# Five more seven-product pairs in the mixing stage of a hybrid decoder layer

## The chip, the cores and the metric

The kernel runs on one core of a Trainium2 chip. The metric is device time in microseconds, the median of several runs; lower is better. TensorE (PE) multiplies matrices, VectorE (DVE) and ScalarE (ACT) do elementwise work, GpSimd (POOL) issues small DMAs here, SyncE (SP) issues the loads of the weights.

## The reference

One decoder layer for 256 tokens of width 2048, in float32:

```
x = x + 1/2 * SwiGLU_1(RMSNorm(x))            # 2048 -> 5632 twice, 5632 -> 2048
z = RMSNorm(x) @ W_in                         # q, k, v and gates of two head groups
o_g = gated linear attention (4 heads), normed, times silu(r)
o_a = dilated attention (8 heads): q and k normed per head, rotary, three windows merged
x = x + concat(o_g, o_a) @ W_out              # 2048 -> 2048
x = x + 1/2 * SwiGLU_2(RMSNorm(x))
```

The weights are far larger than the activations: all in all 350 MB of them are loaded, each once.

## The kernel before, in words

**Products in three parts.** Each float32 weight tile is split into a rounded part (`wh`, made on ACT, L114) and a remainder (`wl`, made on DVE, L115), and so is each activation tile (`hh` and `hl`, or `oah`, `oal`, `ogh`, `ogl`). A product is the sum of three matmuls: high by high (L277), high activation by low weight (L279), low by high (L281). Tokens come in two row tiles of 128 (`t`), output columns in blocks of 512 in pairs (`j`), and the depth in tiles of 128 (`k`), which are loaded in pairs (`kp`): one load of 1 MB brings two depth tiles by two column blocks into a `raw` buffer (three of them).

**Plain pairs.** `column_pair` runs 16 depth tiles into four PSUM banks. One depth tile is one job: a `wh`/`wl` tile of 1024 columns, then 2 x 2 x 3 = 12 matmuls of 512 columns. A pair of depth tiles is 24 matmuls.

**Sevens.** For a pair of depth tiles the two row tiles, two depth tiles and two column blocks make a 2 x 2 by 2 x 2 product of blocks. `seven_products` computes it with seven block products instead of eight (21 matmuls instead of 24), from sums of activation blocks and sums of weight blocks. The sums of activations are made by `seven_forms` (DVE, then a split). The sums of weights are made by `seven` (L234 on), in four parts, "plain", "last", "sums" and "more", each of which gives one `wh`/`wl` tile ("last" only half a tile, in a room of its own). Four of the seven products go to four further PSUM banks (`ms`), which a list of "fold" operations brings to the results after the last seven of the pair: in the output pairs `fold_into_xs` adds them to the residual `xs` with one ACT copy and eight DVE operations.

**Order of the weights.** A list of jobs (L182 to L186) holds all weight tiles in the order of their use. `weights` makes tiles until three are ready; there are four `wh` and four `wl` buffers (`WBUF`). `_order` turns a text such as "ssgsgsss" into an order of plain pairs (s) and sevens (g); the sevens take the first depth pairs, the plain ones the rest. Before the change, ten of the eleven column blocks of a feed-forward part have two sevens each ("ssgssgss"), the down projections have six sevens each, the second output pair has two ("ssgsgsss"), and q, k, v, the gates' projections and the first output pair have none.

**Work beside the matmuls.** `later` is a list of small pieces (rotary turns, scores, gated attention, norms) of which a few run before each step of matmuls, by a plan of `span` steps. A second list (`held`) keeps the ends of the norm blocks until the last seven of the second output pair, because they write the rows of `hh` and `hl` that hold the sums of activations (`lent`). The program is written in this order; the framework then orders each engine's instructions by its own estimate of when they are ready, so pieces move against each other. Waits between engines are semaphores that it sets.

**The stages around the change,** from the trace: q from 676 us, k from 721, v from 763, a narrow projection, three projections for the gated attention, the first output pair from 959, the second from 1005, the second feed-forward part from 1045. During the k pair DVE turns q by its rotary table (`rotate`, L628 to L634). At the end of a pair, `store` writes the banks out scaled (ACT, L651). In the first output pair the first eight depth tiles are attention (`oah`, `oal`), the other eight gated attention (`ogh`, `ogl`), which `gated` finishes in that same stage (L866, L867, transposes L110). After the first output pair, `out_evac` adds the banks to `xs` (L895) and `renorm` starts the norm of these columns: a transpose in 32 x 32 blocks, 16 DMAs for each of four blocks on GpSimd's queue (L136), and later `finish` (L156).

## Time and profile before

| what | value |
|---|---|
| median of 3 runs | 1718.4 us (1717.45 to 1718.85) |
| span of the profiled execution | 1715.9 us |
| PE busy | 1705.4 us, 99%, 7974 matmuls |
| DVE busy | 1416.9 us, 83% |
| ACT busy | 947.1 us, 55% |
| POOL busy | 505.7 us, 29% |
| loads of weights | 350.25 MB, 57.2% of the 16 DMA engines |
| chain that ended last | PE 89%, DMA 4%, DVE 4% |

The profiled execution is one run, and the profile gives its span from the first to the last instruction, which leaves out what lies around it. In rows of the trace a tile is written as `out<-in`, with buffer numbers left out; a number in brackets after a row is the idle time of the engine before it and what ended that. The mean duration of an instruction contains some overlap with its neighbours.

### The profile page before, as it was taken

What the parts mean: (1) busy time and instruction counts of PE and PEld (TensorE: products, weight loads), DVE (VectorE), ACT (ScalarE), POOL (GpSimd) and SP (SyncE); (2) the same over time, 40 slices, a digit from 0 to 9 for tenths busy, and PEclk for the clock granted to TensorE, in tenths of its full rate; (3) what the DMA queues carried; (4) which work ended last, traced back from release to release, by engine and by line L of the source; (5) the groups of instructions that cost most, each with busy time, mean ns of one, the idle gap of its engine ahead of it and who ended that gap; (6) DMA issues with size and microseconds to landing.
All of it is one profiled execution on the core that took longest, in us unless ns stands there. A gap on an engine that the chain in (4) does not pass through costs nothing.

```text
span 1715.9 us, 22309 instructions
## 1 busy us (share of the span) xinstructions
PE 1705.4 (99%) x7974; PEld 1485.1 (87%) x7974; DVE 1416.9 (83%) x1731; ACT 947.1 (55%) x1173; POOL 505.7 (29%) x1002
## 2 busy tenths in 40 slices
PE   9999999999999999999999999999999999999999
PEld 7888888888888888888888888888888888888887
DVE  6888889898898788577865788788888898898876
ACT  7555555555555555564654555555555555555453
POOL 0333334344410611054250043333333333420000
PEclk9999999999999999999999999999999999999999
DMA  8666666556665657577564467666666666665654
GB/s 345 213 229 224 219 211 232 208 213 236 234 250 219 217 203 244 192 237 235 195 210 172 148 198 269 210 231 225 222 224 220 226 212 224 218 242 222 248 204 147
DMA packets 85807, 378.62 MB, mean 221 GB/s; under 512 B 21392, under 2 KB 38800, under 8 KB 42688
## 3 DMA queue, kind: packets, MB, share of 16 engines
q1 hardware_dynamic: 50864, 350.25, 57.2%
q0 software_dynamic: 34112, 25.88, 5.3%
q8 instruction: 62, 1.02, 0.2%
q10 hardware_dynamic: 720, 1.07, 0.2%
q14 instruction: 49, 0.40, 0.1%
HBM read 354.57 MB, written 4.19 MB: 209 GB/s over the span
## 4 chain that ended last, share of the span: by engine, by line
PE 89%; DMA 4%; DVE 4%; POOL 1%; issue 1%; ACT 0%; DVEq 0%; SPq 0%; ACTq 0%; POOLq 0%
PE acc L279 20%; PE acc L277 20%; PE acc L281 20%; PE tp L281 4%; PE tp L277 4%; PE tp L279 4%; PE acc L303 4%; PE acc L304 4%; PE acc L302 4%; DVE wl L115 2%; DMA raw<-in_w_dn_dram 2%; DMA hh<-us 1%; PE tp L303 1%; PE tp L304 1%; PE tp L302 1%
## 5 line engine op out<-in xcount | busy, mean ns | idle before, releaser
L114 ACT ACTIVATE wh<-raw 128x1024 fp32r<-128x1024 f32 (+1 forms) x660 | 683.6, 1048 | 531.2 <-PE acc L281 186.6
L115 DVE TENSOR_TENSOR wl<-raw,wh 128x1024 fp32r<-128x1024 f32 (+1 forms) x658 | 790.3, 1215 | 168.4 <-ACT wh L114 165.0
L136 POOL DMA_DIRECT2D xs<-us x704 | 344.9, 497 | 552.1 <-ACT wh L114 200.3
L281 PE MATMUL acc<-wh,hl 128*128 128x512 f32 x1232 | 370.7, 380 | 0.0
L279 PE MATMUL acc<-wl,hh 128*128 128x512 f32 x1232 | 369.9, 380 | 0.1
L277 PE MATMUL acc<-wh,hh 128*128 128x512 f32 x1232 | 363.5, 381 | 2.6 <-ACT wh L114 2.6
L277 PEld LDWEIGHTS acc<-wh,hh 128*128 128x128 f32 x1232 | 232.3, 189 | 37.7 <-ACT wh L114 4.1
L279 PEld LDWEIGHTS acc<-wl,hh 128*128 128x128 f32 x1232 | 232.6, 189 | 33.9 <-issue 0.7
L281 PEld LDWEIGHTS acc<-wh,hl 128*128 128x128 f32 x1232 | 232.6, 189 | 32.9 <-DVE hl L544 0.2
L279 PE MATMUL acc<-wl,uh 128*128 128x512 f32 x384 | 117.2, 380 | 0.0
L281 PE MATMUL acc<-wh,ul 128*128 128x512 f32 x384 | 117.0, 379 | 0.0
L277 PE MATMUL acc<-wh,uh 128*128 128x512 f32 x384 | 112.1, 380 | 0.7 <-ACT wh L114 0.7
L136 POOL DMA_DIRECT2D hh<-us x128 | 62.4, 506 | 126.7 <-DVE us L129 69.0
L241 DVE TENSOR_TENSOR xs<-raw 128x1024 f32<-128x1024 f32 x40 | 49.0, 1225 | 46.9 <-DMA raw<-in_w_ff_dram 46.9
L277 PEld LDWEIGHTS acc<-wh,uh 128*128 128x128 f32 x384 | 72.3, 189 | 12.0 <-ACT wh L114 1.9
L279 PEld LDWEIGHTS acc<-wl,uh 128*128 128x128 f32 x384 | 72.4, 189 | 10.8 <-DVE wl L115 0.6
L281 PEld LDWEIGHTS acc<-wh,ul 128*128 128x128 f32 x384 | 72.6, 189 | 10.3
L277 PE MATMUL tp<-wh,hh 128*128 128x512 f32 x240 | 73.2, 379 | 0.0
L281 PE MATMUL tp<-wh,hl 128*128 128x512 f32 x240 | 71.4, 379 | 0.0
L279 PE MATMUL tp<-wl,hh 128*128 128x512 f32 x240 | 71.4, 379 | 0.0
L114 ACT ACTIVATE wh<-xs 128x1024 fp32r<-128x1024 f32 x40 | 42.2, 1055 | 45.2 <-PE acc L281 24.1
L114 ACT ACTIVATE swh<-raw 128x512 fp32r<-128x512 f32 x40 | 25.3, 631 | 60.6 <-DMA raw<-in_w_ff_dram 60.6
(326 smaller groups left out, 2382.3 us busy)
## 6 DMA issues: line engine op xcount, KB each, us to landing
raw<-in_w_ff_dram SPq DMA_DIRECT2D x175, 1024.0 KB, 5.0
raw<-in_w_dn_dram SPq DMA_DIRECT2D x88, 1024.0 KB, 4.9
raw<-in_w_mix_dram SPq DMA_DIRECT2D x48, 1024.0 KB, 5.0
raw<-in_w_out_dram SPq DMA_DIRECT2D x16, 1024.0 KB, 4.8
xs<-us POOLq DMA_DIRECT2D x704, 16.0 KB, 3.4
xs<-in_x_dram SPq DMA_DIRECT2D x2, 1024.0 KB, 9.8
xs<-in_x_dram POOLq DMA_DIRECT2D x2, 1024.0 KB, 5.4
hh<-us POOLq DMA_DIRECT2D x128, 16.0 KB, 3.7
```

The lines of the kernel that those rows point to most:

```text
L114: nc.scalar.activation(dst_h, src, AF.Copy)
L115: nc.vector.tensor_sub(dst_l, src, dst_h.bitcast(F32))
L136: nc.gpsimd.dma_start(dst[32 * q:32 * q + 32, ..., r * n:(r + 1) * n], src[32 * r:32 * r + 32, ..., q * n:(q + 1) * n])
L241: nc.vector.tensor_add(room["sum"], b1, mid)
L277: nc.tensor.matmul(ps[j], lhsT=sh, rhs=alt(wh[:, j, :]), start=first and i == 0, stop=False)
L279: nc.tensor.matmul(ps[j], lhsT=sh, rhs=alt(wl[:, j, :]), start=False, stop=False)
L281: nc.tensor.matmul(ps[j], lhsT=sl, rhs=alt(wh[:, j, :]), start=False, stop=last and i == len(ws) - 1)
L302: nc.tensor.matmul(bank, lhsT=a[0], rhs=alt(ws[0][:, j, :]), start=start, stop=False)
L303: nc.tensor.matmul(bank, lhsT=a[0], rhs=alt(ws[1][:, j, :]), start=False, stop=False)
L304: nc.tensor.matmul(bank, lhsT=a[1], rhs=alt(ws[0][:, j, :]), start=False, stop=stop)
```

## The change

The mixing stage gets orders of its own (`MIX_ORDERS`): the pair for k has two sevens. The first output pair becomes a pair with two sevens ("sssgsgss"), the second has three ("sgsgsgss") instead of two. What goes with it:

- `seven` makes its two later sums of weights in rows `room["more"]`, in the part "plain", where such rows are given (k: rows of `kT`; output pairs: `scratch[:, 2:4]`, both also rows of the fold); elsewhere it still makes them in the loaded tile, in the part "sums".
- The sums of activations for k are made in the q pair (before its tiles 10 and 12); those of the output pairs, three now, in the first output pair (before its units 1, 4 and 7).
- The evacuation of k subtracts or adds the folded products on DVE before ACT's store.
- `seven_pair` takes its banks by a list (`first`), can run pieces before a unit (`extra`), can evacuate both row tiles at the end (`after`), and runs all folds that are left in the last unit.
- The gated half is asked for earlier in the first output pair, since its plain pairs now begin with depth pair 2; `evac_r` puts the gate's pieces in the order of the column halves.

```diff
-OUT_ORDERS = [_order("ssssssss"), _order("ssgsgsss")]
+MIX_ORDERS = [_order(t) for t in ("ssssssss", "ssgsgsss", "ssssssss", "ssssssss", "ssssssss", "ssssssss")]
+OUT_ORDERS = [_order("sssgsgss"), _order("sgsgsgss")]
...
                 nc.vector.tensor_add(room["sum"], b1, mid)
+                if "more" in room:
+                    for j, b in enumerate((room["sum"][:, 0, :], room["more"][:, 0, :])):
+                        nc.vector.tensor_add(room["more"][:, j, :], b, raw[:, 1, j, :])
...
             elif part == "sums":
-                for j, b in enumerate((room["sum"][:, 0, :], raw[:, 1, 0, :])):
-                    nc.vector.tensor_add(raw[:, 1, j, :], b, raw[:, 1, j, :])
+                if "more" not in room:
+                    for j, b in enumerate((room["sum"][:, 0, :], raw[:, 1, 0, :])):
+                        nc.vector.tensor_add(raw[:, 1, j, :], b, raw[:, 1, j, :])
...
-                split(wh, wl, raw[:, 1])
+                split(wh, wl, room["more"] if "more" in room else raw[:, 1])
...
-                        if folds:
+                        for _ in range(len(folds) if last else min(1, len(folds))):
                             folds.pop(0)()
...
                 if start:
-                    ms = [acc_bank() for _ in range(4)] if odd is None else four_banks(1 - odd)
+                    ms = [acc_bank() for _ in range(2)] if odd is None else four_banks(1 - odd)
+                    if odd is None:
+                        more = acc_bank if first[2] is tp_bank else tp_bank
+                        ms += [more(), more()]
...
-                        nc.scalar.activation(halves(blk), ps[j], AF.Copy, scale=rt[:, t:t + 1])
+                        src = ps[j]
+                        if rest:
+                            src = halves(blk)
+                            (nc.vector.tensor_add if j else nc.vector.tensor_sub)(src, ps[j], rest[t][j])
+                        nc.scalar.activation(halves(blk), src, AF.Copy, scale=rt[:, t:t + 1])
...
+            forms = {kp: [lent(a, 2 * kp, 1) for a in (oah, oal)] for kp in range(2)}
+            rooms["down"] = {"sum": la, "more": kT[:, :1024].rearrange("p (i f) -> p i f", i=2), "wh": lent(oah, 6, 0), "wl": lent(oal, 6, 0)}
...
+                return [lambda: nc.scalar.activation(p1, m[0], AF.Copy),
+                        lambda: nc.vector.tensor_add(u1, p1, m[2]),
+                        lambda: nc.vector.tensor_add(u2, u1, m[3]),
+                        lambda: nc.vector.tensor_add(v(slice(1, 4, 2)), v(slice(1, 3)), m[1].unsqueeze(1).to_broadcast([P, 2, 2, 256]))]
...
-            column_pair(hacts, store(tok(xk), lambda t, j, b, rs: rotate(1, kTv, t, j, b, rs)))
+            fold, rest = folded(kT.rearrange("p (i f) -> p i f", i=4))
+            seven_pair(hacts, MIX_ORDERS[1], forms, 1, store(tok(xk), lambda t, j, b, rs: rotate(1, kTv, t, j, b, rs), rest), fold)
...
-                    later.append(lambda j=j, sg=sg: gated(t, j, sg))
+                if t:
+                    later.extend([lambda j=j, u=u: gated(u, j, silus[j, u]) for j, u in sorted(silus)])
...
-            rooms["down"] = {"sum": scratch[:, 0:2, :], "wh": lent(hl, 8, 0), "wl": lent(hl, 10, 0)}
-            oforms = {kp: [lent(hh, 2 * kp, 1), lent(hl, 2 * kp, 1)] for kp in range(2)}
+            rooms["down"] = {"sum": scratch[:, 0:2, :], "more": scratch[:, 2:4, :], "wh": lent(hl, 8, 0), "wl": lent(hl, 10, 0)}
...
-            column_pair(oacts, out_evac(0), span=4, due=8, after=True, extra={8 + 3 * kp: lambda kp=kp: sums_of(kp) for kp in range(2)})
+            seven_pair(oacts, OUT_ORDERS[0], oforms, None, out_evac(0), lambda m: fold_into_xs(m, 0, scratch[:, 2:4, :], 1.0),
+                       span=4, first=[acc_bank] * 4, after=True, extra={1 + 3 * kp: lambda kp=kp: sums_of(kp) for kp in range(3)})
+            order[0] = 3
             holding[0] = 1
-            seven_pair(oacts, OUT_ORDERS[1], oforms, None, out_evac(1), lambda m: fold_into_xs(m, 1, scratch[:, 2:4, :], 1.0))
+            seven_pair(oacts, OUT_ORDERS[1], oforms, None, out_evac(1), lambda m: fold_into_xs(m, 1, scratch[:, 2:4, :], 1.0),
+                       first=[acc_bank] * 2 + [tp_bank] * 2)
```

More of the change, by code (lines that the diff above doesn't have):

```diff
@@ L173, in norm_finish, with jobs_of @@
             rsqrt(rt[:, t:t + 1], ssum[:, t:t + 1])
-        def jobs_of(w, orders):
-            for cp, order in enumerate(orders):
+        def jobs_of(w, orders, base=0):
+            for cp, order in enumerate(orders, base):
                 for kp, seven in order:
@@ L182, in layer_kernel @@
         jobs = [*jobs_of(w_ff1, FF_ORDERS), *jobs_of(w_dn1, DOWN_ORDERS)]
-        jobs += [(w_mix, i, k) for i in range(3 * KT // 2) for k in range(2)] + ["low"]
-        jobs += [(w_mix, i, k) for i in range(3 * KT // 2, 3 * KT) for k in range(2)]
+        jobs += [*jobs_of(w_mix, MIX_ORDERS[:3]), "low", *jobs_of(w_mix, MIX_ORDERS[3:], 3)]
         jobs += jobs_of(w_out, OUT_ORDERS)
@@ L327, in seven_forms, with seven_pair @@
             split(*forms, sums)
-        def seven_pair(acts, pairs, forms, odd, evac, fold, span=None, final=False):
-            cs, ms, folds = [acc_bank(), acc_bank(), tp_bank(), tp_bank()] if odd is None else four_banks(odd), None, []
+        def seven_pair(acts, pairs, forms, odd, evac, fold, span=None, final=False, first=None, extra=None, after=False):
+            cs, ms, folds = [f() for f in first] if odd is None else four_banks(odd), None, []
             if odd is not None:
@@ L342, in seven_pair @@
                 u = units[n]
+                if extra and n in extra:
+                    extra[n]()
                 if isinstance(u, tuple):
@@ L356, in seven_pair @@
                         products(cs[2 * t:2 * t + 2], t, now, ws, n == 0, last, ((0,), (1,)) if g > 1 else ((0, 1),))
-                        if last:
-                            evac(t, [c.rearrange("p (a b) -> p b a", b=2) for c in cs[2 * t:2 * t + 2]])
+                        for h in ((0, 1) if t else ()) if after else (t,):
+                            if last:
+                                evac(h, [c.rearrange("p (a b) -> p b a", b=2) for c in cs[2 * h:2 * h + 2]])
                     n += g
@@ L644, in layer_kernel, with store @@
             turned, copied = [], []
-            def store(dst, after=None):
+            def store(dst, after=None, rest=None):
                 def f(t, ps):
@@ L680, in layer_kernel, with folded, fold @@
             moved_q = e123.rearrange("p e t f -> p (e t f)")[:, :2048].rearrange("p (b t f) -> p b t f", b=2, t=NT)
-            column_pair(hacts, store(tok(xq), lambda t, j, b, rs: rotate(0, moved_q, t, j, b, rs)), span=14, due=8)
+            forms = {kp: [lent(a, 2 * kp, 1) for a in (oah, oal)] for kp in range(2)}
+            rooms["down"] = {"sum": la, "more": kT[:, :1024].rearrange("p (i f) -> p i f", i=2), "wh": lent(oah, 6, 0), "wl": lent(oal, 6, 0)}
+            column_pair(hacts, store(tok(xq), lambda t, j, b, rs: rotate(0, moved_q, t, j, b, rs)), span=14, due=8,
+                        extra={10 + 2 * kp: lambda kp=kp: seven_forms(hacts[2 * kp:2 * kp + 2], forms[kp], t512("full"), t512("sums"))
+                               for kp in range(2)})
+            def folded(room):
+                v = lambda i: room[:, i, :].rearrange("p i (b a) -> p i b a", b=2)
+                p1, u1, u2, u3 = [halves(room[:, i, :]) for i in range(4)]
+                def fold(m):
+                    return [lambda: nc.scalar.activation(p1, m[0], AF.Copy),
+                            lambda: nc.vector.tensor_add(u1, p1, m[2]),
+                            lambda: nc.vector.tensor_add(u2, u1, m[3]),
+                            lambda: nc.vector.tensor_add(v(slice(1, 4, 2)), v(slice(1, 3)), m[1].unsqueeze(1).to_broadcast([P, 2, 2, 256]))]
+                return fold, ((u1, p1), (u3, u2))
             kTv = kT.rearrange("p (b t f) -> p b t f", b=2, t=NT)
```

10 lines of the change are left out of this document (6 added, 4 removed).

## The prediction

> **What bounds the kernel now.** I read the first part of the page, then the table of waits for TensorE, then its instructions in order of time inside the mixing stage, then the busy time of every engine by stage.
>
> ```profile
> span 1715.9 us, 22309 instructions
> PE 1705.4 (99%) x7974; PEld 1485.1 (87%) x7974; DVE 1416.9 (83%) x1731; ACT 947.1 (55%) x1173; POOL 505.7 (29%) x1002
> ```
>
> A busy share of 99% can hide slow matmuls, so the next view is what PE (TensorE) waited for in the whole run, with total, number and longest wait:
>
> ```profile
> PE acc L277 <- ACT wh L114: 3.3, 6, 1.7
> PE tp L103 <- DVE warm L100: 1.5, 1, 1.5
> PE tp L303 <- DVE wl L115: 0.6, 1, 0.6
> PE tp L302 <- ACT wh L114: 0.5, 1, 0.5
> PE acc L303 <- DVE wl L115: 0.4, 1, 0.4
> ```
>
> These add up to 6.3 us. Asked by stretch, none of it lies between 640 and 1100 us, where the change is. So there PE is limited by the matmuls themselves. Their pace, from the first and the last row of a stretch of 86 matmuls of 512 columns in the pair for q:
>
> ```profile
> 700.04 0.59 PE L279 MATMUL acc<-wl,hh 128*128 128x512 f32 x2
> 718.61 0.59 PE L281 MATMUL acc<-wh,hl 128*128 128x512 f32 x2
> ```
>
> 18.57 us over 86 is 0.2159 us each. A matmul taken away in this stage is worth 0.216 us, as long as the weights come in time. Who makes them is the other half: each weight tile is rounded by ACT (ScalarE, `wh`, L114) and its remainder taken by DVE (VectorE, `wl`, L115). The stages (k pair, v pair, first output pair, second output pair, first block of the second feed-forward part):
>
> ```profile
> core 0: us, PE busy (x) PEld busy (x) DVE busy (x) ACT busy (x) POOL busy (x), PEclk, DMA share, GB/s
> ...
> 721.20:762.60 41.40, 41.40 (x193) 36.27 (x192) 31.57 (x44) 25.66 (x55) 23.29 (x36) 1.00 0.67 227
> 762.60:802.00 39.40, 39.40 (x184) 34.49 (x184) 31.52 (x46) 22.02 (x49) 18.03 (x30) 1.00 0.66 220
> 958.50:1005.00 46.50, 46.50 (x229) 39.52 (x228) 33.76 (x49) 24.36 (x33) 0.70 (x1) 1.00 0.47 168
> 1005.00:1045.10 40.10, 40.10 (x187) 35.13 (x186) 37.00 (x44) 23.71 (x32) 28.17 (x58) 1.00 0.74 232
> 1045.10:1086.60 41.50, 41.50 (x201) 36.31 (x201) 33.83 (x51) 23.84 (x33) 5.36 (x11) 1.00 0.68 248
> ```
>
> The clock is 1.00 and PE full in every row. DVE has 9.8 us free in the k pair, 12.7 in the first output pair, and 3.1 in the second, which has two sevens already. So the question of this change is whether DVE can pay for five more.
>
> **The matmuls removed.** A plain pair of weight tiles costs 24 matmuls, a seven 21. Two in k, two in the first output pair and one in the second take away 5 x 3 = 15, or 15 x 0.216 = 3.24 us, all on the path that sets the end. Nothing else on PE is added or taken away: transposes, gated-attention and score matmuls stay. Against the profiled execution that is 1715.9 - 3.24 = 1712.7 us of span. The median of the runs is 1718.4, 2.5 above that span; I carry those 2.5 us over unchanged.
>
> **What DVE pays.** Single durations overlap their neighbours by about 0.1 us, so I use the spacing inside unbroken runs:
>
> ```profile
> 573.98 4.62 DVE L115 TENSOR_TENSOR wl<-raw,wh 128x1024 fp32r<-128x1024 f32 x4
> 959.26 1.29 DVE L866 TENSOR_TENSOR sg<-sg,gon 128x512 f32<-128x512 f32 x2 [0.78 <-ACT sg L877]
> 969.12 0.76 DVE L320 TENSOR_TENSOR full<-oah,oal 128x256 f32<-128x256 f32 x2 [1.97 <-PE tp L110]
> 977.76 0.29 DVE L323 TENSOR_TENSOR sums<-full 128x128 f32<-128x128 f32 x1
> 977.97 0.28 DVE L324 TENSOR_TENSOR sums<-full 128x128 f32<-128x128 f32 x1
> ```
>
> With a last one of about 1.23, 1024 columns cost (4.62 - 1.23) / 3 = 1.13 us; 512 cost 0.60 (1.29 less a single 0.69); 256 about 0.34; 128 about 0.21. A plain pair is two splits of 1024, 2.26 us. A seven is a sum of 1024, three splits of 1024, one of 512 and two sums of 512: 4 x 1.13 + 3 x 0.60 = 6.32. So each seven adds 4.06 us of DVE and gives 0.65 us less time to do it in. That the two later sums go to other rows, and are made in the seven's first part, changes their place, not their price; it lets go of the loaded tile earlier, and lets the first product wait 1.2 us longer for nothing but DVE. Forms of the activations: two sums of 256, four of 128, a split of 512: 2.1 us for each seven. Fold in k: two of 512 and one of 1024, 2.3 us; fold in the first output pair: eight of 512, 4.8 us. Evacuation of k: four subtractions or sums of 512, 2.4 us, done as the v pair begins.
>
> By stage, demand against time:
> - q pair: two forms, 4.2 us; DVE is idle for 14.3 us there (the row below). Nothing.
> - k pair: 31.57 + 2 x 4.06 + 2.3 = 42.0 us in 41.4 - 1.3 = 40.1: 1.9 too much.
> - v pair: 31.52 + 2.4 = 33.9 in 39.4. The new wait, ACT's store behind DVE's subtraction, has ACT's next roundings queued behind it; but the v pair takes banks that the folds freed, so PE doesn't wait for the store. Nothing.
> - First output pair: 33.76 + 8.12 + 4.8 + 2.1 = 48.8 in 46.5 - 1.3 = 45.2.
> - Second output pair: 37.00 + 4.06 = 41.1 in 40.1 - 0.65 = 39.45.
> - Both output pairs: 89.9 in 84.65, 5.2 too much.
>
> ACT gains 1.7 us a seven and stays below 30 us in every stage: nothing.
>
> **What the weights made ahead can absorb.** In the q pair the makers run against full buffers:
>
> ```profile
> L115 DVE TENSOR_TENSOR wl<-raw,wh 128x1024 fp32r<-128x1024 f32 x17 | 20.8, 1223 | 14.3 <-ACT wh L114 14.3
> L114 ACT ACTIVATE wh<-raw 128x1024 fp32r<-128x1024 f32 x17 | 18.0, 1057 | 18.4 <-PE acc L281 18.3
> ```
>
> DVE waits for ACT, and ACT for PE to free a buffer. With four buffers and 12 matmuls (2.59 us) a job, a tile is begun three jobs, 7.8 us, before its use and is ready 1.06 + 1.23 us later: a lead of 5.5 us. An excess below 5.5 us costs nothing if DVE wastes no time; what goes beyond it, PE waits for. In the k pair 1.9 fits. In the output pairs 5.2 just fits at full use, so the waste decides. In the second output pair today:
>
> ```profile
> L115 DVE TENSOR_TENSOR wl<-raw,wh 128x1024 fp32r<-128x1024 f32 x17 | 20.6, 1217 | 2.3 <-ACT wh L114 2.1
> ```
> ```profile
> 1000.00:1020.00 20.00, 20.00 (x94) 17.50 (x94) 18.63 (x22) 13.05 (x19) 11.12 (x23) 1.00 0.54 173
> 1020.00:1040.00 20.00, 20.00 (x95) 17.50 (x94) 18.97 (x23) 10.52 (x11) 14.96 (x32) 1.00 0.86 268
> ```
> ```profile
> 1041.24 1.23 DVE L115 TENSOR_TENSOR wl<-raw,wh 128x1024 fp32r<-128x1024 f32 x1 [1.04 <-ACT wh L114]
> 1043.82 0.69 DVE L895 TENSOR_TENSOR xs<-xs,acc 128x512 f32<-128x512 f32 x1 [0.76 <-PE acc L281]
> ```
>
> Of the stage's 3.1 us idle, 1.04 and 0.76 came when the work was done; 1.3 us, 3%, is true waste. A longer queue hides part of it; I take half, 1.5%: 89.9 / 0.985 = 91.3, less 84.65 and 5.5, leaves **1.1 us** for PE to wait. At no waste it is 0 (-0.3), at 6% (18.63 and 18.97 us busy in the two halves of 1000 to 1040 are 94%) 95.6 - 84.65 - 5.5 = 5.5 us. I expect the wait near the end of the second output pair: after the last seven there are 10.4 us of matmuls for four splits (4.5), the fold (4.8) and two norm blocks (2.4), 11.7 in all. The second of these norm blocks is just in time already, made at 1046.16, used by matmuls that start at 1046.43:
>
> ```profile
> 1042.39 0.68 DVE L156 TENSOR_TENSOR hf<-hh,gT 128x512 f32<-128x512 f32 x1
> 1046.16 0.69 DVE L115 TENSOR_TENSOR hl<-hf,hh 128x512 fp32r<-128x512 f32 x1
> ```
> ```profile
> 1046.43 0.59 PE L277 MATMUL acc<-wh,hh 128*128 128x512 f32 x2
> ```
>
> **Two moved steps.** The gated half of the first output pair's activations is used from the fifth tile on, not the ninth. Today the stage starts, the transposes of the gate find a bank (after L858 has read it), and the ninth tile follows, at:
>
> ```profile
> 958.56 0.59 PE L277 MATMUL acc<-wh,oah 128*128 128x512 f32 x2
> 968.43 0.66 PE L110 MATMUL tp<-ident,sg 128*128 128x128 f32 x4
> 984.19 0.68 PE L277 MATMUL acc<-wh,ogh 128*128 128x512 f32 x2
> ```
> ```profile
> 970.77 0.69 DVE L858 TENSOR_TENSOR on<-tp,rs 128x512 f32<-128x512 f32 x1
> ```
>
> From 958.56 to 984.19 are 25.6 us: eight tiles of 2.59, and 4.9 us of gated attention and transposes. The fifth tile then comes at 958.6 + 10.4 plus some part of the 4.9, and its second row tile 1.3 us later, between 970.3 and 975.2. The second gated block is ready at 971.4 plus transposes (0.4) and two passes of 0.6, or 973.0. That costs between nothing (it is early by 2.2) and 2.7 us; most of the 4.9 lies ahead of it, so I take nothing. And the 64 moves of the norms on GpSimd's queue start from the first output pair's evacuation; their first and last, and the last block that they feed:
>
> ```profile
> 1007.58 5.91 POOL L136 DMA_DIRECT2D hh<-us  x12 [36.84 <-issue]
> 1048.15 0.50 POOL L136 DMA_DIRECT2D hh<-us  x1 [0.50 <-DMA hh<-us]
> 1058.84 0.68 DVE L156 TENSOR_TENSOR hf<-hh,gT 128x512 f32<-128x512 f32 x1
> L136 POOL DMA_DIRECT2D hh<-us x54 | 26.3, 510 | 43.2 <-issue 36.8 <-DMA hh<-us 6.3
> L136 POOL DMA_DIRECT2D e<-qkg x32 | 17.0, 538 | 6.5 <-DMA e<-qkg 4.3 <-PE acc L281 2.2
> ```
>
> The last is issued 10 us before that block is taken up, so a start 2 or 3 us later costs nothing. A move takes 510 ns where DVE is busy for 94% of the time, and 538 ns where it is less so. [...] If each move did wait half a split more (0.57 us), 64 would take 36 us longer, 10 of them free, and the time would be near 1742; I give that 1 in 100, inside the slower case.
>
> **Sum.** 1718.4 - 3.24 + 1.1 = **1716.2 us**.
>
> **Rivals.**
> - All hidden: DVE wastes nothing and the order of its work is lucky. 1718.4 - 3.24 = 1715.2. For it: no wait of PE in a stage with DVE at 37.00 of 40.10. Against it: 5.2 us of excess against 5.5 of lead leaves nothing for one late block. 0.30.
> - DVE becomes the bound of the output pairs, slower than before. While a seven's jobs are in the buffers, each of 1.29 us, three jobs ahead are only 3.9 us, a lead of 1.6 instead of 5.5. If that is what is there when the gated chain, the folds and the norms meet, and the waste is 6%, PE waits 95.6 - 84.65 - 1.6 = 9.3 us: 1718.4 - 3.24 + 9.3 = 1724.5. It is slower from 3.24 us of waiting on. For it: the rows of PE's waits name `wl` and `wh` in stages with sevens. Against it: those waits are 0.6 us at most. 0.20, half of it beyond 0.2%.
> - More than 15 matmuls' worth: a shift of the second feed-forward part also removes its short waits, some 0.5 us. 1714.7. 0.05.
>
> **How the numbers follow.** The forecast has 0.45, from 1715.5 to 1718. About 0.2%, 3.44 us, is what a measurement can tell from no change: below 1714.96 is faster, above 1721.84 slower. The saving alone stops short of that line by 0.2 us, so faster has the last rival and a quarter of the hidden case: 0.12. Slower has half of its rival: 0.11. The rest, 0.77, is within. The range from 1714.8 to 1720.4 leaves out about 0.08 below and 0.12 above; its upper part is the 5.5 us end of the waste.
>
> **What would show it.** PE's instructions fall to 7959. DVE shows 97% or more over both output pairs, near 97% in k. PE's table of waits has new rows on `wl`, `wh` or `hl` with about 1 us in all, late in the second output pair or just behind it, and nothing in k. The forecast is wrong if the waits there exceed 3 us, or if DVE idles in the output pairs while PE waits for a bank or a transpose instead.

## The result, and the profile after

The change makes the kernel slower: 1734.8 us (median of 4 runs, 1732.8 to 1738.3) against 1718.6 us beside it, a ratio of 1.0098 with a 95% interval of 1.0084 to 1.0112. The forecast was 1716.2 us. The profiled execution took 1738.3 us, with a span of 1736.5. Ratios leave disturbed runs out; medians are of all runs.

The first part of the page of after:

```profile
span 1736.5 us, 22359 instructions
PE 1711.5 (99%) x7959; PEld 1485.6 (86%) x7959; DVE 1452.1 (84%) x1792; ACT 957.0 (55%) x1188; POOL 511.7 (29%) x1002
```

The 15 matmuls are gone (7974 to 7959), and yet PE is busy for 6 us longer: some matmuls became slower. The table of PE's waits in the whole run (total, number, longest):

```profile
PE tp L752 <- DMA e<-turn: 5.0, 1, 5.0
PE acc L306 <- ACT wh L115: 4.8, 2, 3.6
PE acc L281 <- ACT wh L115: 3.3, 7, 1.3
PE tp L104 <- DVE warm L101: 1.5, 1, 1.5
PE acc L283 <- DVE wl L116: 1.3, 2, 1.1
PE acc L307 <- DVE wl L116: 1.2, 2, 0.9
PE acc L281 <- ACT ogh L115: 1.1, 1, 1.1
```

Two rows are new and large. L752 is the first matmul of the attention values (`values`), far behind the k pair; it waits 5.0 us for the last block of turned probabilities. L306 is a seven of the second output pair, which waits once for 3.6 us, at its start, for a rounded sum of weights. With the smaller ones the waits from 715 to 1060 us come to 13.1 us. The clock in steps of 2 us behind the three places where PE had stood idle longest:

```profile
870.00:872.00 2.00, 2.00 (x12) 2.00 (x11) 0.42 (x1) 1.50 (x3) 2.00 (x5) 0.50 0.35 80
872.00:874.00 2.00, 2.00 (x7) 1.64 (x7) 0.42 (x1) 0.70 (x2) 2.00 (x4) 0.50 0.39 94
874.00:876.00 2.00, 2.00 (x9) 1.63 (x8) 1.23 (x1) 1.72 (x3) 1.73 (x4) 0.72 0.41 98
876.00:878.00 2.00, 2.00 (x17) 1.92 (x16) 1.89 (x2) 2.00 (x4) 0.00 (x0) 1.00 0.11 25
...
996.00:998.00 2.00, 2.00 (x6) 1.59 (x5) 2.00 (x5) 0.00 (x0) 0.00 (x0) 0.50 0.00 0
...
1034.00:1036.00 2.00, 2.00 (x7) 1.57 (x7) 2.00 (x4) 0.62 (x2) 0.58 (x2) 0.62 0.82 226
```

The column behind POOL is the granted clock. It falls to 0.50, or close to it, behind each of the three places. With (1 - clock) x 2 us for each of these steps and of their neighbours, some 6 us of PE are lost to it. From the first matmul of the k pair to the first of the second feed-forward part, the kernel before takes 326.1 us (719.0 to 1045.1) and the changed one 344.1 (720.7 to 1064.8): 18.0 longer although 3.2 us of matmuls are gone, so 21.2 lost. Waits (13.1) and low clock (6) make up 19 of it. The first feed-forward part, which the change doesn't touch, took from 668.4 to 672.5 us in the profiled executions of this study; so I compare this stretch too, besides the medians.

DVE by stage (k pair, v pair, first and second output pair):

```profile
core 0: us, PE busy (x) PEld busy (x) DVE busy (x) ACT busy (x) POOL busy (x), PEclk, DMA share, GB/s
720.70:762.80 42.10, 40.78 (x187) 34.90 (x186) 38.45 (x54) 26.04 (x54) 19.12 (x20) 1.00 0.56 199
762.80:806.20 43.40, 43.40 (x210) 38.23 (x209) 35.56 (x52) 27.62 (x61) 22.86 (x36) 1.00 0.66 221
966.10:1019.50 53.40, 50.40 (x237) 40.50 (x236) 46.23 (x72) 27.76 (x41) 1.39 (x2) 0.97 0.40 143
1019.50:1064.80 45.30, 41.62 (x184) 35.44 (x184) 43.60 (x54) 25.36 (x33) 26.71 (x55) 0.96 0.68 209
```

DVE's work in the two output pairs is 46.23 + 43.60 = 89.83 us; the forecast had priced it at 89.9. The price was right, and PE waited all the same. At the start of the second output pair one sees why in DVE's instructions in order of time:

```profile
1018.70 1.22 DVE L241 TENSOR_TENSOR scratch<-raw 128x1024 f32<-128x1024 f32 x1
1019.84 0.69 DVE L433 SCALAR_TENSOR_TENSOR xs<-scratch,xs 128x512 f32<-128x512 f32 x1
...
1022.78 1.88 DVE L932 TENSOR_TENSOR xs<-xs,acc 128x512 f32<-128x512 f32 x3
...
1026.91 2.49 DVE L130 STREAM_TRANSPOSE us<-xs 128x512 f32<-128x512 f32 x4
...
1029.88 0.69 DVE L244 TENSOR_TENSOR scratch<-scratch,raw 128x512 f32<-128x512 f32 x1
```
```profile
1030.60 1.06 ACT L115 ACTIVATE wh<-scratch 128x1024 fp32r<-128x1024 f32 x1 [2.54 <-DVE scratch L244]
```

DVE has no gap here: between the first sum of weights (1018.70) and the last (1029.88) stand, besides splits, the end of the first pair's fold (L433), four additions to the residual (L932) and four transposes (L130). ACT can only then round the sum, and PE starts at 1031.71.

### The profile page after: what moved, and what is told of

Read it like the earlier page. It is cut to its first block, busy times and chain, and to the rows that moved or that the text cites. A ratio compares the mean times of both kernels' runs of the same rounds, so it can differ in the third digit from the quotient of the medians.

```text
span 1736.5 us, 22359 instructions
## 1 busy us (share of the span) xinstructions
PE 1711.5 (99%) x7959; PEld 1485.6 (86%) x7959; DVE 1452.1 (84%) x1792; ACT 957.0 (55%) x1188; POOL 511.7 (29%) x1002
## 4 chain that ended last, share of the span: by engine, by line
PE 84%; DMA 5%; DVE 5%; issue 4%; POOL 1%; ACT 1%; SPq 0%; DVEq 0%; ACTq 0%; POOLq 0%
PE acc L283 18%; PE acc L281 18%; PE acc L285 18%; PE tp L285 5%; PE tp L283 5%; PE tp L281 5%; PE acc L307 4%; PE acc L308 4%; PE acc L306 4%; DVE wl L116 3%; DMA hh<-us 1%; DMA raw<-in_w_dn_dram 1%; PE tp L307 1%; PE tp L308 1%; PE tp L306 1%
## 5 line engine op out<-in xcount | busy, mean ns | idle before, releaser
L115 ACT ACTIVATE wh<-raw 128x1024 fp32r<-128x1024 f32 (+1 forms) x653 | 675.8, 1048 | 521.4 <-PE acc L285 167.5
L283 PE MATMUL acc<-wl,hh 128*128 128x512 f32 x1192 | 360.1, 382 | 1.2 <-DVE wl L116 1.1
L285 PE MATMUL acc<-wh,hl 128*128 128x512 f32 x1192 | 358.0, 381 | 0.0
L281 PE MATMUL acc<-wh,hh 128*128 128x512 f32 x1192 | 352.4, 381 | 2.2 <-ACT wh L115 1.9
L281 PEld LDWEIGHTS acc<-wh,hh 128*128 128x128 f32 x1192 | 225.1, 189 | 35.5 <-ACT wh L115 2.6
L283 PEld LDWEIGHTS acc<-wl,hh 128*128 128x128 f32 x1192 | 225.1, 189 | 34.4 <-DVE wl L116 2.3
L285 PEld LDWEIGHTS acc<-wh,hl 128*128 128x128 f32 x1192 | 225.4, 189 | 32.6 <-issue 0.5
L281 PE MATMUL tp<-wh,hh 128*128 128x512 f32 x264 | 80.6, 379 | 0.0
L283 PE MATMUL tp<-wl,hh 128*128 128x512 f32 x264 | 78.5, 379 | 0.0
L169 POOL TENSOR_TENSOR rs<-a,mhalf 128x4 f32<-128x4 f32 (+1 forms) x12 | 19.9, 1657 | 131.5 <-DVE a L631 131.5
```

The source lines that it names most:

```text
L115: nc.scalar.activation(dst_h, src, AF.Copy)
L169: nc.gpsimd.tensor_tensor(dst, src, mhalf[:, :src.shape[-1]], op=ALU.pow)
L281: nc.tensor.matmul(ps[j], lhsT=sh, rhs=alt(wh[:, j, :]), start=first and i == 0, stop=False)
L283: nc.tensor.matmul(ps[j], lhsT=sh, rhs=alt(wl[:, j, :]), start=False, stop=False)
L285: nc.tensor.matmul(ps[j], lhsT=sl, rhs=alt(wh[:, j, :]), start=False, stop=last and i == len(ws) - 1)
```

## The experiments

Three things were open: whether the k pair and the output pairs lose time each by themselves, what makes the values late, and what the output pairs can hold. "Stretch" below is the one from k to the second feed-forward part, 326.1 us before. In what was written ahead of the first four runs, theory A is the one drawn from the two long waits above; B and C are its rivals.

**1. The k pair alone.** `OUT_ORDERS` and what belongs to them as in the kernel before.

```diff
-OUT_ORDERS = [_order("sssgsgss"), _order("sgsgsgss")]
+OUT_ORDERS = [_order("ssssssss"), _order("ssgsgsss")]
```

> Two sevens in the pair for k alone, output pairs as before (6 matmuls fewer, -1.3 us). Theory A, each stage pays for its own late VectorE work: the k pair loses some 1.4 us on weights, and the attention values behind it wait about 5 us for their turned scores and then run some 3 us slower at half clock: about 1718.6 - 1.3 + 9.5 = 1727, with that wait in the table. Rival B, the k pair's delay carries on through the whole mixing stage into the output pairs: about 1734 with waits in the output pairs too. Rival C, only the output pairs cost: about 1717.5.

Measured: 1725.4 us, 1.0039 (1.0025 to 1.0054), stretch 333.2. The values wait 4.3 us.

**2. The output pairs alone.** k plain.

```diff
-MIX_ORDERS = [_order(t) for t in ("ssssssss", "ssgsgsss", "ssssssss", "ssssssss", "ssssssss", "ssssssss")]
+MIX_ORDERS = [_order(t) for t in ("ssssssss", "ssssssss", "ssssssss", "ssssssss", "ssssssss", "ssssssss")]
```

> Output pairs as changed (two and three sevens), k plain (9 matmuls fewer, -1.9 us). Theory A: the waits of the output pairs (3.1 and 3.6 us) and the half clock behind them stay: about 1718.6 - 1.9 + 10 = 1727. Rival B: without the k pair's delay the waits in the output pairs are gone, about 1717. Rival C: about 1733.

Measured: 1724.5 us, 1.0034 (1.0022 to 1.0045), stretch 332.5. The seven waits 3.4 us, and no wait of the values is left. So each place costs about 7 us by itself, and the two add up to 13.9 of the 16.2. Theory A was 1.6 and 2.5 us too high; B and C miss both runs by 7 us and more.

**3. Two sevens in each output pair, and 4. three in the second and none in the first,** k plain in both.

```diff
-OUT_ORDERS = [_order("sssgsgss"), _order("sgsgsgss")]
+OUT_ORDERS = [_order("sssgsgss"), _order("ssgsgsss")]
```
```diff
-OUT_ORDERS = [_order("sssgsgss"), _order("sgsgsgss")]
+OUT_ORDERS = [_order("ssssssss"), _order("sgsgsgss")]
```

> Output pairs with two sevens each, the second in its old order, k plain (6 matmuls fewer, -1.3 us). Theory A: only the first output pair's own waits stay (about 3 us and 2 of half clock), and part of the backlog handed on: about 1722 to 1725. Rival: the third seven of the second pair is what overloads: about 1718.

> Three sevens in the second output pair, first pair and k plain (3 matmuls fewer, -0.65 us). If the 3.6 us wait of the second pair is its own (41.1 us of VectorE in 39.5): about 1718.6 - 0.65 + 3 to 5 = 1721 to 1723. If it is the backlog from the first pair: 1718.0, with no wait over 1 us.

Measured: 1720.4 us, 1.0011 (1.0001 to 1.0021), stretch 327.4, longest wait 0.8; and 1718.3 us, 0.9999 (0.9990 to 1.0009), stretch 325.4. Three sevens in the second pair bring their 0.65 us if the first pair has none. Neither order loses much; both together do. Run 4 came out as the handed-on backlog has it; run 3 lies between its theory (1722 to 1725) and the rival (1718).

**5. The values later,** in the kernel of run 1. Their matmuls come after the decays and the scaled gates of the gated attention; they then read rows that the decays have overwritten, so the values are computed from other numbers.

```diff
-            later.extend([lambda: None] * 2 + [lambda h=h: both(values, h) for h in (0, 2)])
+            later.extend([lambda: None] * 4)
...
                     later.extend([lambda: None] * (n - t % 2) + [lambda f=f, t=t: f(t)])
+                    if f in (scaled, intra):
+                        later.append(lambda h=4 * (f is intra) + 2 * t: both(values, h))
```

> This is the k pair's sevens alone (output pairs as before) with the matmuls of attention values put later in PE's order: heads 0 to 7 after the decays and scaled gates of the gated attention instead of before them. The k sevens alone took 1725.4 us, with a wait of 4.3 us of values for the last turned block and a low clock behind it. Theory (a chain that DVE made late meets a fixed place in PE's order): the wait of 4.3 us and the low clock behind it go, about 2.5 us of lost clock with it, and the time falls to 1718 to 1719.5 us. Rival (DVE has too much work from k to the gates, wherever PE waits for it): the lost time turns up as waits for weights or at the next use, and the time stays at 1723 to 1726 us.

Measured: 1729.6 us, 1.0066 (1.0053 to 1.0079): slower still. The wait of the values is gone, but PE waits 2.5 us at 867 us for a bank that ACT can't empty: its target (`qkg`) is still read by the moves of the same late scores. So the scores, not the place of the values, are late. This run also pushed the gated attention into the first output pair (63.7 us long instead of 46.4), so its total tells nothing more.

**6. The three sevens of the second output pair later,** k plain. **7. The later sums made late and in the loaded tile again,** k plain.

```diff
-OUT_ORDERS = [_order("sssgsgss"), _order("sgsgsgss")]
+OUT_ORDERS = [_order("sssgsgss"), _order("ssgsggss")]
```
```diff
-            rooms["down"] = {"sum": scratch[:, 0:2, :], "more": scratch[:, 2:4, :], "wh": lent(hl, 8, 0), "wl": lent(hl, 10, 0)}
+            rooms["down"] = {"sum": scratch[:, 0:2, :], "wh": lent(hl, 8, 0), "wl": lent(hl, 10, 0)}
```

> Output pairs as changed but with the three sevens of the second pair later: s s g s g g s s instead of s g s g s g s s; the k pair plain. With the changed order this took 1724.5 us with one wait of 3.4 us for a rounded sum at the start of the second output pair. Theory (DVE is behind only there, with the folds, the eight additions to the residual and the transposes of the first pair): the wait of 3.4 us falls under 1 us, the time is 1718 to 1720 us. Rival (two and three sevens are more DVE work than the two pairs hold): a wait of 2 to 4 us moves to the later sevens and the time stays 1723 to 1726 us.

> Output pairs as changed, but the second sums of weights are made late and in the raw buffer, as in the kernel before, not early in the idle fold rows; the k pair plain. With the sums in the fold rows: 1724.5 us. Theory (DVE is simply busy at the start of the second output pair): two additions of 0.7 us less stand ahead of the first split, so the wait of 3.4 us shrinks by at most 1.4 us: 1722.5 to 1725 us. Rival (the fold rows are shared, so the sums wait for the fold of the pair before): the wait of 3.4 us is gone, 1718 to 1720 us.

Measured: 1729.8 us, 1.0056 (1.0042 to 1.0071), and 1730.7 us, 1.0071 (1.0057 to 1.0085). PE's waits from the second output pair on, in run 6:

```profile
PE acc L281 <- ACT hh L115: 3.5, 1, 3.5
PE acc L306 <- ACT wh L115: 0.6, 1, 0.6
```

The wait for the sum is gone, and one of the same length stands at the first block of the second feed-forward part, which waits for the normed activations (`hh`), the last product of the same DVE work. My theory that DVE is behind only at one spot falls; its rival, too much work, had the wait move on, though only as far as the later sevens, and not a time this long. In run 7 both waits are there (3.0 us in three, 2.9 us for `hh`): neither my theory nor the rival expected that. The early sums in the idle rows help; they are not the cause. The profiled executions, 1726.3 and 1729.3 us, were shorter than these medians.

**8. DVE held up on purpose** in the kernel before: 49 idle operations ahead of six weight tiles of the second feed-forward part.

```diff
+HELD = {12: 5, 28: 6, 44: 7, 52: 8, 60: 10, 76: 13}
...
+            held_up = HELD.get(i, 0) if w is w_ff2 else 0
+            for _ in range(held_up if k == 0 else 0):
+                got = raw[:, 0].bitcast(F32)
+                nc.vector.tensor_tensor(got, got, got, op=ALU.max)
```

> The kernel before with 5, 6, 7, 8, 10 and 13 idle operations of DVE (the larger of a raw half and itself, 1024 columns, about 1.2 us each) ahead of one weight tile in six blocks of the second feed-forward part, nothing else changed. The weights' lead of about 5.5 us takes up the first four or so. Theory (a long idle stretch costs PE its clock as well): stretches of idle under 2.5 us are followed by the full clock, those of 3.4 us and more by about 3 to 5 us at half clock (a matmul every 0.43 us), so that each costs its idle time and 1.5 to 2.5 us more. Rival (the low clock seen after the waits belongs to those stages and their small matmuls): the clock stays at 1.0 after every stretch.

Measured, one run: 1778.0 us, 59.7 more, and 49 x 1.22 us are 59.8. The first five (6.1 us) cost PE 0.7 us of waiting, so a lead of some 5 us was there. At the later stalls it was smaller or missing: 6 operations (7.3 us) cost 3.1 us of waiting, 7 (8.5 us) 6.3, 8 (9.8 us) 7.0, 10 (12.2 us) 12.4 and 13 (15.9 us) 16.2. Why it was missing there isn't shown. In all PE waited 45.7 us. PE around the stall of 10 operations, then the clock behind the first stall and behind this one:

```profile
1373.39 0.48 PE L307 MATMUL acc<-wh,fh 128*128 128x512 f32 x1 [2.26 <-ACT wh L115]
...
1385.46 1.22 PE L282 MATMUL acc<-wh,hh 128*128 128x512 f32 x2 [9.56 <-ACT wh L115]
```
```profile
1100.00:1108.00 8.00, 7.16 (x32) 5.63 (x32) 6.09 (x7) 6.01 (x7) 6.21 (x13) 1.00 0.72 240
...
1386.00:1389.00 3.00, 3.00 (x8) 2.35 (x7) 3.00 (x4) 2.25 (x3) 0.00 (x0) 0.50 0.22 30
1389.00:1392.00 3.00, 3.00 (x15) 2.61 (x14) 1.81 (x2) 1.06 (x1) 0.00 (x0) 0.97 0.82 336
```

So the low clock belongs to idle time and not to the mixing stage. It lasts some 3.7 us here, and costs half of that. All six stalls took 59.7 us, some 14 more than the waits. The rival, full clock after every stall, falls; but the theory's limit of 2.5 us, below which the full clock should stay, was the author's estimate, and it doesn't hold either: a wait of 2.35 us at 1184 us was followed by the half clock (granted clock 0.50 from 1185 to 1190 us).

**9. One seven in the k pair, and 12. only the copy ahead of the store of k,** without a seven.

```diff
-MIX_ORDERS = [_order(t) for t in ("ssssssss", "ssgsgsss", "ssssssss", "ssssssss", "ssssssss", "ssssssss")]
+MIX_ORDERS = [_order(t) for t in ("ssssssss", "sssgssss", "ssssssss", "ssssssss", "ssssssss", "ssssssss")]
```
```diff
+                        src = halves(blk)
+                        nc.vector.tensor_copy(src, ps[j])
+                        nc.scalar.activation(halves(blk), src, AF.Copy, scale=rt[:, t:t + 1])
```

The first edit is made in the kernel of run 1, the second in the kernel before, and for k alone.

> One seven instead of two in the k pair (s s s g s s s s), output pairs as in the kernel before. With two: 1725.4 us, a wait of 4.3 us of attention values for the last turned block. Theory (DVE's surplus of work in the k pair makes the chain from k to the values late by some 10 us, of which the values' place in PE's order has under 4 us to spare): with 4.1 us less on DVE the chain is late by about 5 us, the wait shrinks to 0 to 1.5 us, no low clock follows, and the time is 1717.5 to 1719.5 us. Rival (it is the fixed part, the fold and the subtraction ahead of the store of k, that makes it late): the wait stays at 3 us or more, 1722 to 1725 us.

> The kernel before, with one change: the four blocks of k are first copied from PSUM by DVE, and ACT scales that copy, as behind the fold, but without sevens or fold in the k pair. Theory (backlog): the pass alone makes the chain 2 to 3 us later, within the 3 to 4 us that the values have to spare: no wait over 0.5 us, 1717.5 to 1719.5 us. Rival (the pass is what makes it late): a wait of values of 2 to 4 us, 1721 to 1724 us.

Measured: 1721.1 us, 1.0014 (1.0006 to 1.0023), with a wait of 2.4 us and a low clock behind it, where 0 to 1.5 us and none was expected; and 1718.6 us, 1.0005 (0.9996 to 1.0013), without one. The copy is free, as both the forecast and the theory had it. But the backlog theory doesn't fit run 9. For four kernels, the last move of k on GpSimd, the full scores of the first heads on PE, and the values: the kernel before,

```profile
L136 POOL DMA_DIRECT2D kT<-e x16: 533/536/549, 797.2 to 812.0; - x16
```
```profile
824.75 1.03 PE L700 MATMUL tp<-kT,qT 128*128 128x256 f32 x4
```
```profile
859.33 0.38 PE L721 MATMUL tp<-e,va 128*128 128x128 f32 x2
```

run 9 (one seven),

```profile
L137 POOL DMA_DIRECT2D kT<-e x16: 533/533/549, 799.8 to 811.6; - x16
```
```profile
828.52 1.03 PE L731 MATMUL tp<-kT,qT 128*128 128x256 f32 x4
```
```profile
863.55 0.46 PE L752 MATMUL tp<-e,va 128*128 128x128 f32 x2 [2.45 <-DMA e<-turn]
```

and run 1 (two sevens):

```profile
L137 POOL DMA_DIRECT2D kT<-e x16: 533/536/549, 806.8 to 820.4; - x16
```
```profile
835.47 1.03 PE L731 MATMUL tp<-kT,qT 128*128 128x256 f32 x4
```
```profile
867.43 0.77 PE L752 MATMUL tp<-e,va 128*128 128x128 f32 x2 [4.34 <-DMA e<-turn]
```

In run 9 the last move of k is issued no later than before (811.6 against 812.0), yet the scores start 3.8 us later (counted from the start of the k pair, the moves 0.3 and the scores 4.5 us later). They wait for nothing there: they stand later in PE's queue, behind 3745 main matmuls instead of 3726, and in run 1 behind 3765. The values hardly move with them: 3864, 3873, 3870. The framework orders PE's instructions by its own estimate of when they are ready. The new theory is that DVE's new work changed that estimate for the scores, not for the values, and that this order makes the values wait. Runs 13, 15 and 16 test the order; the estimate itself is not on record.

**10. Two and two sevens with 3.7 us of idle work** on DVE ahead of the second output pair's first plain tile (an edit of run 3). **11. One seven in k, three in the second output pair,** none in the first.

```diff
+            if w is w_out and i == 10 and k == 0:
+                got = raw[:, 0].bitcast(F32)
+                for _ in range(3):
+                    nc.vector.tensor_tensor(got, got, got, op=ALU.max)
```
```diff
-MIX_ORDERS = [_order(t) for t in ("ssssssss", "ssgsgsss", "ssssssss", "ssssssss", "ssssssss", "ssssssss")]
-OUT_ORDERS = [_order("sssgsgss"), _order("sgsgsgss")]
+MIX_ORDERS = [_order(t) for t in ("ssssssss", "sssgssss", "ssssssss", "ssssssss", "ssssssss", "ssssssss")]
+OUT_ORDERS = [_order("ssssssss"), _order("sgsgsgss")]
```

> Two sevens in each output pair (1720.4 us so far, waits of 0.8 and 0.4 us) with three idle operations of DVE (1.2 us each, 3.7 us, a little under the price of a seven) ahead of the first plain tile of the second output pair; the k pair plain. Theory (the output pairs have room for four sevens and no more on DVE, and the lead of weights is no room, because the second feed-forward part needs it again): waits of 3 to 4.5 us appear in the second pair or at the start of the feed-forward part, with a low clock behind the long ones: 1723.5 to 1726 us. Rival (the third seven of the second pair waits on its own early sums): the lead takes the 3.7 us up, 1720 to 1721.5 us.

> One seven in the k pair, three in the second output pair, none in the first: two sevens more than the kernel before in all, 1.3 us of matmuls less. Theory: none of the two places has a surplus over 1 us, no wait over 1 us, 1716.5 to 1718.5 us. Rival (any seven more in the k pair costs more than it brings): 1719 us or more.

Measured: 1724.4 us, 1.0035 (1.0024 to 1.0047), 4.0 us more than run 3 for 3.7 us of DVE work (2.6 us more in the stretch of the profiled execution, whose 1721.8 us are the shortest of the six); the waits are 2.2 us and four of 0.8 us or less, and the clock stays at 1.00 behind them. And 1722.7 us, 1.0023 (1.0015 to 1.0032), a miss: the values wait 1.8 us (the order of PE again), and 2.2 us more of waits are spread over the second output pair and the start of the feed-forward part.

The kernel before and runs 4, 3, 10 and 2, both output pairs together:

```profile
sum 86.50, PE 86.50 PEld 74.58 DVE 70.76 ACT 47.98 POOL 28.87; mean PE 43.25 PEld 37.29 DVE 35.38 ACT 23.99 POOL 14.43
```
```profile
sum 85.90, PE 85.90 PEld 74.05 DVE 75.71 ACT 49.56 POOL 30.88; mean PE 42.95 PEld 37.02 DVE 37.85 ACT 24.78 POOL 15.44
```
```profile
sum 87.90, PE 86.64 PEld 73.15 DVE 82.57 ACT 51.60 POOL 26.36; mean PE 43.32 PEld 36.57 DVE 41.28 ACT 25.80 POOL 13.18
```
```profile
sum 90.40, PE 86.98 PEld 73.09 DVE 85.27 ACT 50.28 POOL 26.06; mean PE 43.49 PEld 36.55 DVE 42.63 ACT 25.14 POOL 13.03
```
```profile
sum 93.00, PE 88.19 PEld 73.64 DVE 88.40 ACT 53.19 POOL 27.59; mean PE 44.10 PEld 36.82 DVE 44.20 ACT 26.60 POOL 13.80
```

The first number is the length of the two pairs. With 0.65 us added for each seven more than before (one, two, two, three), the time lost is 0.0, 2.7, 5.2 and 8.4 us for 75.7, 82.6, 85.3 and 88.4 us of DVE work. Between runs 3, 10 and 2 each us of DVE's work costs about a us of time; carried back to no loss, this line starts at some 80 us. Length less DVE's work is what DVE stood idle: 10.2 us in run 4, and 5.3, 5.1 and 4.6 in runs 3, 10 and 2. It got below that in none of them. (Some 1.7 us of run 2's loss is the low clock behind its wait of 3.4 us.)

**13. Run 1 with the scores kept early in PE's order; 15. run 9 likewise.** The next main matmul is pinned behind the scores.

```diff
-                        nc.tensor.matmul(ps[j], lhsT=sh, rhs=alt(wh[:, j, :]), start=first and i == 0, stop=False)
+                        mm = nc.tensor.matmul(ps[j], lhsT=sh, rhs=alt(wh[:, j, :]), start=first and i == 0, stop=False)
+                        if pin and pin.pop():
+                            tc.keep_in_program_order(mm)
...
+                pin[:] = [True]
...
+            later.extend([lambda: None] * 7)
             for h in range(0, AH, 2):
-                later.append(lambda h=h: both(scores, h))
-                if h == 2:
-                    later.append(lambda: None)
-            later.extend([lambda: None] * 2 + [lambda h=h: both(values, h) for h in (0, 2)])
+                later.extend([lambda h=h: both(scores, h), lambda: None])
+            later.extend([lambda: None] * 3 + [lambda h=h: both(values, h) for h in (0, 2)])
```

`pin` is set behind the matmuls of each head's scores.

> The k pair's two sevens alone (1725.4 us, wait of 4.3 us of values), with the matmuls of scores 24 to 45 main matmuls earlier in PE's order (a main matmul is kept behind them) and everything else as it was, the values at the same place. Theory (the order of PE's instructions, which the framework sets by its own estimate, put the scores 39 matmuls later than in the kernel before, more than k is late, and the values only 6): the scores start 6 to 8 us earlier, the wait of values shrinks to 0 to 1 us, no low clock, 1717 to 1719.5 us. Rival (k itself is too late, by DVE's backlog and the pass ahead of its store): PE or DVE waits for kT at the scores and the values still wait 3 us or more, 1722 to 1726 us.

> One seven in the k pair (1721.1 us, wait of values 2.4 us), with the scores earlier in PE's order in the same way. There k's turned blocks were issued as early as in the kernel before, but the scores stood 19 matmuls later. Theory of the order: no wait of values, 1716.8 to 1718.5 us. Rival (backlog): 1720 us or more with a wait of 2 us.

Measured: 1719.5 us, 1.0009 (1.0000 to 1.0019), stretch 327.1 instead of 333.2; and 1718.7 us, 1.0002 (0.9994 to 1.0011), just above its range, stretch 325.1 instead of 329.6. In run 13:

```profile
L137 POOL DMA_DIRECT2D kT<-e x16: 536/536/549, 805.9 to 820.3; - x16
```
```profile
827.48 1.03 PE L734 MATMUL tp<-kT,qT 128*128 128x256 f32 x4
```
```profile
862.30 0.46 PE L756 MATMUL tp<-e,va 128*128 128x128 f32 x2
```

k is as late as in run 1 (820.3 and 820.4), the scores come 8.0 us earlier (6.6 counted from the start of the k pair), behind 3732 main matmuls, and the values wait for nothing. With k equally late, the order alone made the difference. The rival, that k itself is too late, falls.

**14. Two pinned sevens in k and three in the second output pair,** none in the first; the edit of runs 13 and 15 on the changed kernel with

```diff
-OUT_ORDERS = [_order("sssgsgss"), _order("sgsgsgss")]
+OUT_ORDERS = [_order("ssssssss"), _order("sgsgsgss")]
```

> Two sevens in the k pair with the scores kept early, and three sevens in the second output pair, none in the first: nine main matmuls fewer than the kernel before. If both theories hold (the order for k, the amount of DVE's work for the output pairs): waits under 2 us in all, 1716 to 1718.5 us. If DVE's backlog in the k pair counts by itself: 1722 us or more.

Measured: 1720.0 us, 1.0009 (0.9999 to 1.0018), stretch 326.4: a miss by 1.5 us at the upper end. The single waits are 1.1 us and less.

**16. The whole change with the scores pinned; 17. the same less one seven,** two in the second output pair. Run 16 is the changed kernel with the edit of runs 13 and 15 and no other; run 17 has besides

```diff
-OUT_ORDERS = [_order("sssgsgss"), _order("sgsgsgss")]
+OUT_ORDERS = [_order("sssgsgss"), _order("ssgsgsss")]
```

> The whole change with nothing but the scores kept early in PE's order. The whole change takes 1734.8 us, 16.2 more than the kernel before; k alone costs 7.4, the output pairs alone 6.5, which leaves some 2.3 for the two together (the values and the gated attention behind them, late from k, run into the first output pair). If the order of the scores is k's whole cost and the source of that rest, 6 us of k and the 2.3 go: 1725 to 1728 us, with the wait of 3.5 us at the start of the second output pair still there. If the rest belongs to DVE's work in the output pairs: 1728 to 1731 us.

> The whole change less one seven: two sevens in k with the scores kept early, two sevens in each output pair, so 12 main matmuls fewer than the kernel before. From the single runs (k with the scores kept early 2.0 us over the kernel before, two and two 1.9 to 2.4): 1720 to 1723 us, no wait of PE over 1.5 us. If the two places still add to each other: 1724 us or more.

Measured: 1725.1 us, 1.0040 (1.0028 to 1.0052), and 1723.0 us, 1.0026 (1.0017 to 1.0034). With the scores early in the order, 9.7 of the whole change's 16.2 us are gone. Some 8 of them are accounted for: k's own part (5.9, run 1 against run 13) and what the two halves measured alone had left over (2.3). The wait at the start of the second output pair shrank too, which wasn't expected: 2.2 us without a low clock, instead of 3.6 with it. What stays is in the main the output pairs' surplus (6.5 alone, run 2). No version is faster than the kernel before by more than the measurement tells; the best, runs 4 and 15, are equal to it as far as the measurement tells.

## Why the prediction was wrong

- **The matmuls removed:** right. 15 are gone, and where nothing else is lost one seven shortens the stretch by about its 0.65 us (run 4: 0.7, run 15: 1.0).
- **What DVE pays:** right in the output pairs: 89.83 us measured, 89.9 forecast. That it is right to 0.1 us is luck: in run 2, with the same sevens and less of the gated attention in these pairs, it is 88.40. In the k pair 38.45 us were measured against 42.0; 1.7 of the missing 3.5 us are in the v pair (35.56 against 33.9), the rest was not placed.
- **"An excess below 5.5 us costs nothing if DVE wastes no time":** this step failed for the output pairs. A lead of some 5 us was there at the first stall of run 8, but less of it and then nothing at the later ones, and it wasn't there here: the table of runs 4, 3, 10 and 2 loses about a us for a us from 80 us of DVE work in some 85, where the forecast let the loss begin at 84.65 + 5.5 = 90.15 if DVE never idles. The norm blocks at the end of the stage (run 6) need DVE to be done in time, and a lead of weights doesn't serve them; that this is the reason is argued, not tested by itself. The waste was mis-sized as well: DVE stood idle for 4.6 to 5.3 us of the two pairs, 5 to 6%, where the sum took 1.5%. The forecast's rival with DVE as the bound had the mechanism and gave 1724.5 us; the output pairs alone took 1724.5. The equal figure is in part luck, since the rival counted the k pair's 1.3 us of matmuls as saved too. It had a chance of 0.20.
- **"In the k pair 1.9 fits", "v pair: nothing":** PE did wait only 1.4 us in the k pair and not at all in the v pair. What was left out is that the kernel's order isn't fixed by the text: the sum treated the scores and values as standing where they stood, and the framework moved the scores 39 main matmuls back. Early scores take 9.7 us off the whole change (after against run 16), and no rival named it. That the order costs the time is shown; why the framework chose it is not.
- **The price of a wait:** the forecast charged idle time only. The low clock behind the long waits added 6 us to 13.1.
- **"Two moved steps":** the gated half cost one wait of 1.1 us where nothing was taken, inside its bounds of 0 to 2.7. GpSimd's moves of the norms didn't grow with DVE's load, and no run shows the wait of half a split for each move that the case of 1742 us takes; the group in after is

```profile
L137 POOL DMA_DIRECT2D hh<-us x62 | 30.1, 498 | 55.0 <-PE acc L308 43.1 <-DMA hh<-us 8.9 <-issue 2.9
```

498 ns each with DVE busy for 96% of the second output pair, 510 before.
- **What would show it:** 7959 matmuls came. DVE at 97% or more did not: it is 91% busy in both output pairs together (89.83 of 98.7 us) and 91% in the k pair. Of the two signs of being wrong the first came, single waits of more than 3 us. The second, DVE idle while PE waits for a bank or a transpose, did not: while PE waited in the output pairs (6.6 us in five waits, for `wh`, `ogh` and `hh`), DVE was busy for all but 0.2 us. It idled before that (7.2 of 53.4 us in the first output pair), and half of this in one stretch that ended with the transposes of the gate, right ahead of PE's waits:

```profile
983.46 0.76 DVE L324 TENSOR_TENSOR full<-oah,oal 128x256 f32<-128x256 f32 x2 [3.77 <-PE tp L111]
```

Still open: whether runs 16 and 17 lose more than their parts. Their profiled first output pair is 54.6 us long instead of 47.6, since more of the gated attention falls into it (242 matmuls instead of 222); that this, too, is the framework's order was not tried. In the ratios little of it is left: 1.0026 for run 17 against 1.0011 and 1.0009 for runs 3 and 13, and 1.0040 for run 16 against 1.0034 and 1.0009 for runs 2 and 13.

## What to carry to other kernels

Where a framework orders the queues by its own estimate, compare the order of the two programs before summing costs: look for a chain of small matmuls whose first half moves and whose second doesn't. A lead of prepared tiles is at best a buffer for a stall, not room for work: sum the maker's work over the whole stage against its time, with the idle time that it never got below (4.6 to 5.3 us here) taken off, not a lead added. And a wait of PE of some 2.4 us or more can cost more than itself (2.35 us in run 8 and 2.45 in run 9 had the half clock behind them): 13.1 us of waits brought 6 us of low clock in the changed kernel, 45.7 brought some 14 in run 8.

## What the runs showed of the hardware

A matmul of 512 columns started every 0.43 us behind the long waits, against 0.2159 in the rows of the prediction; in after, behind the 5.0 us:

```profile
872.58 0.63 PE L283 MATMUL acc<-wl,hh 128*128 128x512 f32 x1
873.01 0.63 PE L285 MATMUL acc<-wh,hl 128*128 128x512 f32 x1
873.44 0.63 PE L281 MATMUL acc<-wh,hh 128*128 128x512 f32 x1
```

It lasted from 869.5 to 875.1 us there, 5.6 us, and some 3.7 us behind the stall of 10 operations in run 8. No single length of the wait decides whether it follows. One of 2.35 us in run 8 was followed by it, and so was one of 2.45 us in run 9; one of 2.2 us in run 10 wasn't, nor was one of 2.46 us in run 5. Runs 9 and 5, the wait and a stretch behind it (the granted clock is 0.53 and 1.00):

```profile
863.55 0.46 PE L752 MATMUL tp<-e,va 128*128 128x128 f32 x2 [2.45 <-DMA e<-turn]
866.00:868.00 2.00, 2.00 (x7) 1.59 (x6) 0.42 (x1) 1.05 (x2) 2.00 (x5) 0.53 0.41 98
```
```profile
867.75 0.48 PE L281 MATMUL acc<-wh,hh 128*128 128x512 f32 x1 [2.46 <-ACT qkg L829]
868.00:870.00 2.00, 2.00 (x10) 1.74 (x10) 0.00 (x0) 2.00 (x5) 2.00 (x5) 1.00 0.39 91
```

Short waits were followed by it in one run and not in another: in run 16 PE was busy for 2.34 of the 4 us from 980 to 984, with no single wait of more than 1.3 us, and the granted clock of the next 4 us was 0.68; in run 17 it was busy for 2.20 of the 4 us from 982 to 986, likewise with no wait of more than 1.3 us, and the clock of the next 4 us was 1.00. What decides it is not shown by any run.
